# A split-precision decoder layer: the products with the weights' lower parts are issued behind those with the upper parts

## The chip, the cores and the metric

The kernel runs on one core of a Trainium2 chip. The metric is the device time of one execution in microseconds. A profile of one execution stands beside it; its span runs from the first to the last instruction of the program. The engines are named as in the profile: PE is TensorE (matrix products), PEld its weight loads, DVE is VectorE, ACT is ScalarE, POOL is GpSimd, SP issues most of the DMAs.

## What is computed

One decoder layer for 256 tokens with 2048 channels, in float32: a conditioned RMSNorm, an input projection to twelve wide parts, two kinds of attention (retention with 4 heads, HGRN2 with 8), their output projections, gates and a merge, and then a feed-forward block with a causal convolution and a down projection from 5632 channels. Cut to its products:

```python
h   = modulate(rms_norm(x, g_norm1), shift1, scale1)
p   = h @ w_in                                   # 2048 x 12288
y_a = (o_r * silu(rg)) @ w_ret_o                 # 1024 x 2048
y_b = (o_h * silu(hg)) @ w_hg_o                  # 1024 x 2048
x   = x + gate1 * ((sigmoid(ga) * y_a + sigmoid(gb) * y_b) @ w_out)
h2  = modulate(rms_norm(x, g_norm2), shift2, scale2)
u   = causal_depthwise_conv(h2 @ w_up, conv_w, conv_b)
a, b = split(u)
x   = x + gate2 * ((silu(a) * b) @ w_down)       # 5632 x 2048
out = rms_norm(x, g_final)
```

## The kernel before

**Split operands.** The products keep more bits than one pass of the reduced-precision type fp32r holds: each operand is split into an upper part, rounded to fp32r, and a lower part, the rest. A product of two split operands is made of three: upper by upper, upper by lower and lower by upper. The activations are split once (tiles `hT`, `og`, `mT`, `gs`): columns 0 to 255 of such a tile are the upper part for 256 tokens (`act[:, :T]`), columns 256 to 511 the lower part (`act[:, T:]`). The weights come from HBM in float32 and are split on the way, piece by piece.

**Pieces of weights.** A piece is a pair of k tiles (128 rows of the weight matrix each) by a group of 512 columns, or a single k tile where only one is left. `load` (L153) issues its DMA on SP into one of 12 buffers `raw`; `upper` (L159) has ACT round it into `wh` (L167); `rest` (L170) has DVE subtract that from `raw`, which gives `wl` (L172). There are four buffers each of `wh` and `wl`. `pieces` (L176) yields them one after another, and `products` (L213) has a function `mm` issue the products for each k tile as it comes.

**Two forms of product.** Where the result is to have tokens as rows, `mm_rows` (L190) is used: the activations are the stationary operand, a token tile of 128 at a time, and the 512 weight columns move. For each k tile and each of the two token tiles it issues three products into that token tile's own PSUM bank: L196 (upper activations, `wh`), L197 (upper activations, `wl`), L198 (lower activations, `wh`). Where the result is to have channels as rows, `mm_cols` (L200) is used: a block of 128 weight columns is stationary, and the 256 tokens move. For each k tile and each of four blocks it issues L209 (`wh`, upper), L210 (`wh`, lower), L211 (`wl`, upper); two blocks share a PSUM bank. A pair of k tiles is twelve products of 512 columns in `mm_rows`, and twenty-four of 256 columns in `mm_cols`.

**Stages.** (1) `run` starts with four column groups at k tiles 0 and 1, issued one k tile at a time (L800 to L819), while the rest of the activations is still being made. (2) The twelve attention groups (L836 to L864): column groups for the retention's and HGRN2's queries and keys, row groups for the values; few k tiles at a time, and in between. (3) Gates and branch gates as row groups (L874 to L893), while the attention itself runs as generators (`hgrn` L521, `retention` L700) whose steps `pump` (L127) puts between the pieces; their matrix products are small and stand between the pairs on PE. (4) The output projections (L897, L913, L931), rows. (5) The up projection (`up_group`, L1066), which has products of its own (L1081 with `wh`, L1083 with `wl`) and does not call `mm_rows` or `mm_cols`. (6) The down projection (`down`, L1104), rows.

**Order.** A planner in the tile framework lays down the order of instructions on each engine when the program is built: it takes what is ready by its own estimate, in program order, when several are. Instructions given to `pin` (L141) keep program order among themselves while `self.ordered` is set. The products of `mm_rows` and `mm_cols` are not pinned; products into the same PSUM bank keep their order. Buffers come free for the next writer when the last reader is done, so ACT's next `wh` waits for the last product that reads the old one.

**Held products.** With `hold`, the last k tiles of a group are not issued as they come, but kept in `held` and then issued for token tile 0 first and token tile 1 after (L223 to L225), so that the work on token tile 0 can start ahead. This is done in the last group of the output projection and in the last group of the down projection.

Of the kernel before, what the change touches and what calls it, by code (L numbers as in the profile page):

```python
# [19 lines left out]
P = 128  # L20
D = 2048
T = 256
NT = T // P
# [10 lines left out]
RESIDENT = 2  # L34
# [21 lines left out]
class Kernel:  # L56
# [130 lines left out]
            uppers[k // 2] = None  # L187
            yield [(k + j, wh[:, j, :], wl[:, j, :]) for j in range(m)]

    def mm_rows(self, ps, act, wh, wl, first, last, tiles=range(NT)):  # L190

        nc = self.nc
        for t in tiles:
            hi = act[:, t * P : (t + 1) * P]
            lo = act[:, T + t * P : T + (t + 1) * P]
            nc.tensor.matmul(ps[t], lhsT=hi, rhs=wh, start=first, stop=False)  # L196
            nc.tensor.matmul(ps[t], lhsT=hi, rhs=wl, start=False, stop=False)  # L197
            nc.tensor.matmul(ps[t], lhsT=lo, rhs=wh, start=False, stop=last)  # L198

    def mm_cols(self, ps, act, wh, wl, first, last):  # L200

        nc = self.nc
        hi, lo = act[:, :T], act[:, T:]
        for j in range(4):
            cs = slice(j * P, (j + 1) * P)

            opens = first and j % 2 == 0
            out = ps[j // 2][:, j % 2 * T : (j % 2 + 1) * T]
            nc.tensor.matmul(out, lhsT=wh[:, cs], rhs=hi, start=opens, stop=False, skip_group_check=True)  # L209
            nc.tensor.matmul(out, lhsT=wh[:, cs], rhs=lo, start=False, stop=False, skip_group_check=True)  # L210
            nc.tensor.matmul(out, lhsT=wl[:, cs], rhs=hi, start=False, stop=last, skip_group_check=True)  # L211

    def products(self, mm, ps, src, act, k0, kts, hold=0, first=True, last=True, gain=None):  # L213

        held = []
        for step in self.pieces(src[:, k0 : k0 + kts, :], kts, gain):
            for kt, wh, wl in step:
                if kt >= kts - hold:
                    held.append((kt, wh, wl))
                else:  # L220
                    mm(ps, act(k0 + kt), wh, wl, first and kt == 0, last and kt == kts - 1)
            self.pump(len(step) / 2)
        for t in range(NT if held else 0):  # L223
            for kt, wh, wl in held:
                mm(ps, act(k0 + kt), wh, wl, kt == 0, kt == kts - 1, [t])  # L225
        return ps

    def rows(self, src, act, k0=0, kts=KT, ps=None):
# [526 lines left out]
    def run(self):  # L755
        nc, a = self.nc, self.a
# [11 lines left out]
        def act(k):  # L768
            return hT[k // 2][:, k % 2, :]
# [13 lines left out]
        mms = [self.mm_rows if c0 in ROWS else self.mm_cols for c0 in ATT]  # L783
# [15 lines left out]
        ps = [self.po2(), self.po2(), self.pg(), self.pg()][:FIRST]  # L799
        for k in range(2):  # L800
            for i in range(4 if k else 1):
                if k and i == 1:
                    self.times(k, 1, rx)
                next(ada[k])
            if k == 0:
                self.times(k, 1, rx)

            ahead = 2 * k
            uppers = [self.upper(a["wa"][g][:, k : k + 1, :], 1, G) for g in range(ahead + 1)]
            rests = [self.rest(z) for z in uppers[:ahead]]  # L810
            for _ in ada[k]:
                pass
            for g in range(FIRST):
                if g >= ahead:
                    rests.append(self.rest(uppers[g] if g < len(uppers) else self.upper(a["wa"][g][:, k : k + 1, :], 1, G)))
                wh, wl = rests[g]
                if k == g == 0:
                    self.pin(nc.scalar.activation(rx_sb, rx, AF.Copy))
                mms[g](ps[g], act(k), wh[:, 0, :], wl[:, 0, :], k == 0, k == 1 and g >= RESIDENT)  # L819
        for _ in range(2):  # L820
            next(ada[2])
        self.ordered = False
# [10 lines left out]
        g = FIRST  # L833
        att, gates = [], []
        small = False
        while min(done) < KT:  # L836
# [25 lines left out]
            g = (g + 1) % len(ATT)  # L862
            if have == KT and done[0] < KT:
                g = min(i for i in range(len(ATT)) if done[i] < KT)  # L864
# [9 lines left out]
        for j in range(4):  # L874
            ps = self.rows(a["wb"][j], act)
# [55 lines left out]
        for j in range(4):  # L931
            last = j == 3
            x1.append(self.load_rows(j))
            if not last:
                g = self.row(self.gate["gate1"], j, "g1")
            if j == 2:
                g3 = self.row(self.gate["gate1"], 3, "g1")
            elif last:
                g = g3
            ps = self.products(self.mm_rows, self.po2() if last else self.pg(), a["wout"][j], actm, 0, KT, hold=4 * last, gain=g if last else None)  # L940
            if last:
                g = None
# [305 lines left out]
```

## Time and profile before

| | |
|---|---|
| median of 3 runs | 1516.57 us (1516.51 to 1517.36) |
| span of the profiled execution | 1514.7 us |
| PE busy | 1498.0 us |
| PEld busy | 1288.4 us |
| DVE busy | 1205.9 us |
| ACT busy | 845.4 us |

The profile's page gives no time of its own for the profiled execution beside its span; the median lies 1.87 us above that span. Busy times of one engine count overlapping instructions once. A weight load overlaps the product in front of it. In rows that list groups of instructions, the columns are line, engine, operation, written tile and read tiles, shape, count, then busy microseconds and mean nanoseconds of one, then the idle time of the engine ahead of them with what ended it. In the timeline, the first column is the start in microseconds from the beginning of the span and the second the time the rows take. In the table by stretches the columns are the length, then busy time and count of PE, PEld, DVE, ACT and POOL, the granted TensorE clock, the DMA share and GB/s.

### The profile page before, as it was taken

The page shows a single profiled execution, that of the slowest core. Times are in us where ns is not written, and L with a number is a line of the kernel's source. Part 1 is how long each engine was busy: PE and PEld are TensorE (multiplying, and loading weights), DVE is VectorE, ACT ScalarE, POOL GpSimd, SP SyncE. Part 2 cuts the span into 40 slices and gives each one's busy share as a digit, 9 for nine tenths or more (in the row PEclk, how much of TensorE's full clock was granted, in tenths as well). Part 3 has the DMA queues.
Part 4 walks back from the last instruction along what each step waited for, and adds up shares of the span by engine and source line. Part 5 has one row for each costly group of instructions (what it writes and reads, how often), then busy time and mean ns, then how long its engine had stood idle before and what let it go on. Part 6 is the DMA issues. An engine that isn't in the chain of part 4 may idle for free.

```text
span 1514.7 us, 23095 instructions
## 1 busy us (share of the span) xinstructions
PE 1498.0 (99%) x8722; PEld 1288.4 (85%) x8722; DVE 1205.9 (80%) x1639; ACT 845.4 (56%) x1207; POOL 4.0 (0%) x8
## 2 busy tenths in 40 slices
PE   8999999999999999999999999999999999999997
PEld 6999999878788888888888888888888888888886
DVE  7899996898999877898977778778777769455694
ACT  6645454768775644445466555555555558344343
POOL 0000000000000000000000000000000000000000
PEclk9999999999999999999999999999999999999999
DMA  9999997777888889989847777777777666667651
GB/s 376 377 344 332 316 325 228 229 275 266 287 264 289 275 288 329 320 289 358 310 133 242 237 230 233 228 233 231 230 245 228 220 187 196 201 209 215 177 178 56
DMA packets 110997, 385.75 MB, mean 255 GB/s; under 512 B 12803, under 2 KB 13347, under 8 KB 110885
## 3 DMA queue, kind: packets, MB, share of 16 engines
q1 hardware_dynamic: 110016, 383.14, 76.7%
q8 instruction: 68, 1.11, 0.3%
q10 hardware_dynamic: 868, 1.13, 0.2%
q14 instruction: 45, 0.36, 0.1%
HBM read 382.11 MB, written 2.11 MB: 254 GB/s over the span
## 4 chain that ended last, share of the span: by engine, by line
PE 95%; ACT 2%; DVE 1%; DMA 1%; issue 0%; SPq 0%; DVEq 0%; ACTq 0%
PE pg L196 13%; PE pg L197 13%; PE pg L198 13%; PE po L1081 11%; PE pg L1081 10%; PE po L1083 5%; PE pg L1083 5%; PE po L197 3%; PE po L198 3%; PE po L196 3%; PE pg L209 3%; PE pg L211 3%; PE pg L210 3%; PE po L209 1%; PE po L210 1%; PE po L211 1%
## 5 line engine op out<-in xcount | busy, mean ns | idle before, releaser
L167 ACT ACTIVATE wh<-raw 128x1024 fp32r<-128x1024 f32 (+1 forms) x536 | 550.6, 1033 | 523.2 <-PE pg L198 183.4
L172 DVE TENSOR_TENSOR wl<-raw,wh 128x1024 fp32r<-128x1024 f32 (+1 forms) x536 | 634.5, 1190 | 248.2 <-ACT wh L167 247.4
L421 DVE SCALAR_TENSOR_TENSOR raw<-raw,sc 128x1024 f32<-128x1024 f32 x192 | 233.5, 1219 | 0.0
L1081 PE MATMUL po<-h2T,wh 128*128 128x512 f32 x704 | 221.1, 395 | 0.0
L1081 PE MATMUL pg<-h2T,wh 128*128 128x512 f32 x688 | 216.4, 396 | 0.0
L196 PE MATMUL pg<-wh,hT 128*128 128x512 f32 x512 | 203.1, 397 | 0.2 <-ACT p L789 0.2
L197 PE MATMUL pg<-wl,hT 128*128 128x512 f32 x512 | 200.5, 392 | 1.7 <-DVE wl L172 1.7
L198 PE MATMUL pg<-wh,hT 128*128 128x512 f32 x512 | 199.6, 390 | 0.0
L1083 PEld LDWEIGHTS po<-h2T,wl 128*128 128x128 f32 x704 | 132.2, 188 | 31.3
L1083 PEld LDWEIGHTS pg<-h2T,wl 128*128 128x128 f32 x688 | 129.1, 188 | 31.0 <-DVE wl L172 0.5
L1083 PE MATMUL po<-h2T,wl 128*128 128x256 f32 x704 | 138.3, 278 | 0.0
L1083 PE MATMUL pg<-h2T,wl 128*128 128x256 f32 x688 | 135.3, 278 | 0.1
L197 PEld LDWEIGHTS pg<-wl,hT 128*128 128x128 f32 x512 | 96.2, 188 | 22.1 <-DVE wl L172 3.3
L198 PEld LDWEIGHTS pg<-wh,hT 128*128 128x128 f32 x512 | 96.1, 188 | 20.2
L196 PEld LDWEIGHTS pg<-wh,hT 128*128 128x128 f32 x512 | 96.2, 188 | 19.9 <-ACT p L789 0.4
L211 PE MATMUL pg<-hT,wl 128*128 128x256 f32 x384 | 109.0, 284 | 0.6 <-DVE wl L172 0.6
L209 PE MATMUL pg<-hT,wh 128*128 128x256 f32 x384 | 109.2, 284 | 0.1
L210 PE MATMUL pg<-hT,wh 128*128 128x256 f32 x384 | 109.0, 284 | 0.0
L1081 PEld LDWEIGHTS po<-h2T,wh 128*128 128x128 f32 x704 | 107.1, 189 | 0.0
L1081 PEld LDWEIGHTS pg<-h2T,wh 128*128 128x128 f32 x688 | 104.7, 189 | 0.0
L211 PEld LDWEIGHTS pg<-hT,wl 128*128 128x128 f32 x384 | 74.0, 193 | 0.8 <-DVE wl L172 0.8
L209 PEld LDWEIGHTS pg<-hT,wh 128*128 128x128 f32 x384 | 74.1, 193 | 0.6 <-ACT wh L167 0.2
(250 smaller groups left out, 2208.3 us busy)
## 6 DMA issues: line engine op xcount, KB each, us to landing
raw<-in_wup SPq DMA_DIRECT2D x176, 512.0 KB, 4.5
raw<-in_wdown SPq DMA_DIRECT2D x88, 512.0 KB, 4.3
raw<-in_wa SPq DMA_DIRECT2D x80, 512.0 KB, 6.0
raw<-in_ada SPq DMA_DIRECT2D x64, 512.5 KB, 5.7
raw<-in_ada SPq DMA_DIRECT2D x64, 512.0 KB, 5.8
raw<-in_wab SPq DMA_DIRECT2D x64, 512.0 KB, 5.1
raw<-in_gate SPq DMA_DIRECT2D x32, 512.5 KB, 4.8
raw<-in_wb SPq DMA_DIRECT2D x32, 512.0 KB, 5.0
```

What stands on the lines that cost most here:

```text
L167: self.pin(self.nc.scalar.activation(wh, raw, AF.Copy))
L172: self.last = self.nc.vector.tensor_tensor(wl, raw, wh.bitcast(F32), ALU.subtract)
L196: nc.tensor.matmul(ps[t], lhsT=hi, rhs=wh, start=first, stop=False)
L197: nc.tensor.matmul(ps[t], lhsT=hi, rhs=wl, start=False, stop=False)
L198: nc.tensor.matmul(ps[t], lhsT=lo, rhs=wh, start=False, stop=last)
L209: nc.tensor.matmul(out, lhsT=wh[:, cs], rhs=hi, start=opens, stop=False, skip_group_check=True)
L210: nc.tensor.matmul(out, lhsT=wh[:, cs], rhs=lo, start=False, stop=False, skip_group_check=True)
L211: nc.tensor.matmul(out, lhsT=wl[:, cs], rhs=hi, start=False, stop=last, skip_group_check=True)
L421: dot = self.pin(nc.vector.scalar_tensor_tensor(raw[:, 0, :], raw[:, 0, :], 1.0, self.sc[:, u * GW : u * GW + w], ALU.mult, ALU.mult, accu ...
L1081: self.pin(nc.tensor.matmul(ps[j + z], lhsT=wh[:, cs[z]], rhs=act, start=kt == 0, stop=False, skip_group_check=bool(begun)))
L1083: nc.tensor.matmul(ps[j + z][:, :T], lhsT=wl[:, cs[z]], rhs=act[:, :T], start=False, stop=kt == KT - 1, skip_group_check=bool(begun))
```

## The change

`mm_rows` and `mm_cols` take the k tiles of a piece together, as a list of items, instead of one k tile a call. They issue the products with `wh` first (with the activations' upper part and then the lower part), for all items and both token tiles or all four column blocks, and the products with `wl` behind them. `products` hands them the whole piece. The held products of a token tile are issued the same way, all with `wh` and then all with `wl`. The number of products, their operands and the banks that they add into are the same. `up_group` is not touched.

```diff
-    def mm_rows(self, ps, act, wh, wl, first, last, tiles=range(NT)):
+    def mm_rows(self, ps, items, first, last, tiles=range(NT)):
 
         nc = self.nc
         for t in tiles:
-            hi = act[:, t * P : (t + 1) * P]
-            lo = act[:, T + t * P : T + (t + 1) * P]
-            nc.tensor.matmul(ps[t], lhsT=hi, rhs=wh, start=first, stop=False)
-            nc.tensor.matmul(ps[t], lhsT=hi, rhs=wl, start=False, stop=False)
-            nc.tensor.matmul(ps[t], lhsT=lo, rhs=wh, start=False, stop=last)
+            hi, lo = [slice(u * T + t * P, u * T + (t + 1) * P) for u in range(2)]
+            for i, (act, wh, _) in enumerate(items):
+                nc.tensor.matmul(ps[t], lhsT=act[:, hi], rhs=wh, start=first and i == 0, stop=False)
+                nc.tensor.matmul(ps[t], lhsT=act[:, lo], rhs=wh, start=False, stop=False)
+        for t in tiles:
+            hi = slice(t * P, (t + 1) * P)
+            for i, (act, _, wl) in enumerate(items):
+                nc.tensor.matmul(ps[t], lhsT=act[:, hi], rhs=wl, start=False, stop=last and i == len(items) - 1)
...
-    def mm_cols(self, ps, act, wh, wl, first, last):
+    def mm_cols(self, ps, items, first, last):
 
         nc = self.nc
-        hi, lo = act[:, :T], act[:, T:]
-        for j in range(4):
-            cs = slice(j * P, (j + 1) * P)
-
-            opens = first and j % 2 == 0
-            out = ps[j // 2][:, j % 2 * T : (j % 2 + 1) * T]
-            nc.tensor.matmul(out, lhsT=wh[:, cs], rhs=hi, start=opens, stop=False, skip_group_check=True)
-            nc.tensor.matmul(out, lhsT=wh[:, cs], rhs=lo, start=False, stop=False, skip_group_check=True)
-            nc.tensor.matmul(out, lhsT=wl[:, cs], rhs=hi, start=False, stop=last, skip_group_check=True)
+        cs = [slice(j * P, (j + 1) * P) for j in range(4)]
+        outs = [ps[j // 2][:, j % 2 * T : (j % 2 + 1) * T] for j in range(4)]
+        for i, (act, wh, _) in enumerate(items):
+            for j in range(4):
+
+                opens = first and i == 0 and j % 2 == 0
+                nc.tensor.matmul(outs[j], lhsT=wh[:, cs[j]], rhs=act[:, :T], start=opens, stop=False, skip_group_check=True)
+                nc.tensor.matmul(outs[j], lhsT=wh[:, cs[j]], rhs=act[:, T:], start=False, stop=False, skip_group_check=True)
+        for i, (act, _, wl) in enumerate(items):
+            for j in range(4):
+                nc.tensor.matmul(outs[j], lhsT=wl[:, cs[j]], rhs=act[:, :T], start=False, stop=last and i == len(items) - 1, skip_group_check=True)
 
     def products(self, mm, ps, src, act, k0, kts, hold=0, first=True, last=True, gain=None):
 
         held = []
         for step in self.pieces(src[:, k0 : k0 + kts, :], kts, gain):
-            for kt, wh, wl in step:
-                if kt >= kts - hold:
-                    held.append((kt, wh, wl))
-                else:
-                    mm(ps, act(k0 + kt), wh, wl, first and kt == 0, last and kt == kts - 1)
+            items = [(act(k0 + kt), wh, wl) for kt, wh, wl in step]
+            kt = step[0][0]
+            if kt >= kts - hold:
+                held += items
+            else:
+                mm(ps, items, first and kt == 0, last and kt + len(step) == kts)
             self.pump(len(step) / 2)
         for t in range(NT if held else 0):
-            for kt, wh, wl in held:
-                mm(ps, act(k0 + kt), wh, wl, kt == 0, kt == kts - 1, [t])
+            mm(ps, held, hold == kts, True, [t])
         return ps
...
-                mms[g](ps[g], act(k), wh[:, 0, :], wl[:, 0, :], k == 0, k == 1 and g >= RESIDENT)
+                mms[g](ps[g], [(act(k), wh[:, 0, :], wl[:, 0, :])], k == 0, k == 1 and g >= RESIDENT)
```

## The prediction

> **What bounds the kernel now.** I read the page first: busy time, the chain that ended last, the groups.
>
> ```profile
> span 1514.7 us, 23095 instructions
> ...
> PE 1498.0 (99%) x8722; PEld 1288.4 (85%) x8722; DVE 1205.9 (80%) x1639; ACT 845.4 (56%) x1207; POOL 4.0 (0%) x8
> ...
> PE 95%; ACT 2%; DVE 1%; DMA 1%; issue 0%; SPq 0%; DVEq 0%; ACTq 0%
> ```
>
> TensorE is busy for 1498.0 of 1514.7 us and is 95% of the chain. The change removes no product and adds none, so two things can move the time: what one product costs, and the 16.7 us in which TensorE is idle, with what hides inside its busy time. For the first I read the groups with shapes kept apart.
>
> ```profile
> L198 PE MATMUL pg<-wh,gs 128*128 128x512 f32 x176 | 68.6, 390 | 0.0
> L196 PE MATMUL pg<-wh,gs 128*128 128x512 f32 x176 | 68.5, 389 | 0.0
> L197 PE MATMUL pg<-wl,gs 128*128 128x512 f32 x176 | 68.5, 389 | 0.0
> ```
>
> In the down projection nothing waits, and the three products of a k tile cost the same to 1 ns, whichever stands first and whichever operand it reads. A new order of the same three is therefore worth nothing by itself. For the second I read who waited for whom on PE, then the timeline around each wait for `wl`.
>
> ```profile
> PE pg L197 <- DVE wl L172: 1.7, 3, 0.8
> ...
> PE pg L211 <- DVE wl L172: 0.6, 1, 0.6
> ```
>
> That is 2.3 us in four waits, for the lower part of a weight piece, which DVE makes (L172) out of the upper part, which ACT makes (L167). The four places, PE alone:
>
> ```profile
> 38.34 0.28 PE L210 MATMUL pg<-hT,wh 128*128 128x256 f32 x1
> 39.17 0.39 PE L211 MATMUL pg<-hT,wl 128*128 128x256 f32 x1 [0.55 <-DVE wl L172]
> 39.40 0.28 PE L209 MATMUL pg<-hT,wh 128*128 128x256 f32 x1
> ...
> 281.74 0.28 PE L211 MATMUL pg<-hT,wl 128*128 128x256 f32 x1
> 281.86 0.39 PE L196 MATMUL pg<-wh,hT 128*128 128x512 f32 x1
> 282.73 0.50 PE L197 MATMUL pg<-wl,hT 128*128 128x512 f32 x1 [0.48 <-DVE wl L172]
> 283.07 0.39 PE L198 MATMUL pg<-wh,hT 128*128 128x512 f32 x1
> ...
> 375.68 0.39 PE L198 MATMUL pg<-wh,hT 128*128 128x512 f32 x1
> 375.90 0.39 PE L196 MATMUL pg<-wh,hT 128*128 128x512 f32 x1
> 376.66 0.50 PE L197 MATMUL pg<-wl,hT 128*128 128x512 f32 x1 [0.38 <-DVE wl L172]
> 377.00 0.40 PE L198 MATMUL pg<-wh,hT 128*128 128x512 f32 x1
> ...
> 384.73 0.39 PE L196 MATMUL pg<-wh,hT 128*128 128x512 f32 x1
> 385.93 0.50 PE L197 MATMUL pg<-wl,hT 128*128 128x512 f32 x1 [0.81 <-DVE wl L172]
> 386.26 0.39 PE L198 MATMUL pg<-wh,hT 128*128 128x512 f32 x1
> ```
>
> Starts, not durations, show the pace, as products overlap: undisturbed, a 512-column product starts 0.22 to 0.23 us after the one before (375.68 to 375.90) and a 256-column one 0.12 (281.74 to 281.86). I take 0.227 and 0.12. A stall costs more than its idle time, because the pipeline drains and the product behind the stalled one starts 0.33 to 0.34 us later instead of 0.227. From starts: at 39 us 0.83 - 0.12 and 0.23 - 0.12, together 0.82; at 282 us 0.87 - 0.23 and 0.34 - 0.23, 0.75; at 376 us 0.76 - 0.23 and 0.34 - 0.23, 0.64; at 385 us 1.20 - 0.23 and 0.33 - 0.23, 1.07. **Sum 3.28 us.** The rest of the idle time is the start-up (before 17 us, and small waits for hT), the hand-over to the up projection and what follows the last product: none of it waits for `wl`.
>
> **The change part by part.** *Order inside a pair.* In mm_rows the first product with `wl` was second of twelve; it becomes ninth, 7 x 0.227 = 1.59 us later after the pair's start. In mm_cols with a pair it goes from third to seventeenth, 14 x 0.12 = 1.68 us. The four waits last 0.38 to 0.81 us, so all would be covered if `wl` comes when it comes now: -3.28 us. Ends for this term: 2.3 us (idle time alone) and 3.28. I take 3.28, since the drag behind each stall is in the rows.
>
> *What is late next.* The tightest place is the last. If the wait at 376 us goes, the pairs start at 375.90, 378.62, 381.34 and 384.06 (12 x 0.227 = 2.72 us each); the fourth is the one that started at 384.73. It needs this:
>
> ```profile
> 382.94 1.04 ACT L167 ACTIVATE wh<-raw 128x1024 fp32r<-128x1024 f32 x1
> ```
>
> ```profile
> 384.67 1.20 DVE L172 TENSOR_TENSOR wl<-raw,wh 128x1024 fp32r<-128x1024 f32 x1
> ```
>
> `wh` is done at 383.98, 0.08 us ahead of 384.06; `wl` at 385.87, where the ninth product comes at 384.06 + 1.82 = 385.88. So this place is covered with nothing to spare. It stays out of the sum, and makes a rival.
>
> *Buffers.* `wh` is read for the last time at product 8 of 12 instead of 12 of 12, so its buffer comes free 4 x 0.227 = 0.91 us sooner; ACT waits for just that:
>
> ```profile
> ACT wh L167 <- PE pg L198: 183.4, 131, 2.6
> ```
>
> `wl` is read until product 12 instead of 11, 0.23 us later. DVE does not feel it: it needs the new `wh` too, which with 1.04 us of ACT ends at 1.82 + 1.04 = 2.86 us, behind the pair's end at 2.72. In a stretch where TensorE never waits the earlier `wh` is worth nothing; before an attention burst it is up to 0.9 us more lead. Below nothing it can only go through the planner (third rival). The loads on SP's queue go by `raw`, which DVE frees after `wl`, at most 0.9 us sooner: nothing, as no product waits for them.
>
> *Tokens' lower part.* In mm_rows it is needed second instead of third, 0.23 us sooner. No product of a row group waits for it, so 0. act() of a pair's second tile is called ahead of the first tile's products; each call that emits work emits it for the whole pair already, so nothing moves.
>
> *Held pieces, end.* For one token tile the held products are the same in number; the last starts where it did. Up projection (L1081, L1083): untouched. 0.
>
> *Stationary operand.* L196 and L197 load the same tokens one behind the other; the new order separates them.
>
> ```profile
> L197 PEld LDWEIGHTS pg<-wl,hT 128*128 128x128 f32 x512 | 96.2, 188 | 22.1 <-DVE wl L172 3.3
> ```
>
> There are as many loads as products (8722 each), L197's are not shorter for following L196, and 188 ns lie under a pace of 227: 0. The Trainium skill, "TensorE: Matmul & The Clock Gate", section "Step-by-step: what each phase is for", speaks against the change here: weights that stay put are to be loaded once and multiplied repeatedly. By that rule 1120 spared loads would be lost, at 188 ns 211 us if they stood in the open; the trace spares none today.
>
> *Sum.* 1514.7 - 3.3 = 1511.4 for the profiled execution. The median of the runs, 1516.57, lies 1.87 us above the span; the same distance gives **1513.3**, 0.22% less. About 0.2%, 3.0 us, is what a measurement of this kernel can tell from no change, so the forecast stands on that line.
>
> **The rivals.** *The wait comes back as a wait for `wh`* (0.32). For: the margins of 0.08 and 0.01 us above; a product that is late at the start of a pair is not helped by the new order. If the waits at 376 and 385 us return in full, 0.64 + 1.07 are lost again and 1.57 stays: 1515.0. Against: `wh` buffers come free sooner.
>
> *It does nothing* (0.08): the planner that lays down each engine's order puts the products back, or lead gained at a place is used up by the next burst: 1516.6.
>
> *Slower: DVE's order* (0.15). The planner works with its own estimate of when a buffer comes free. Sooner free `wh` changes which of ACT's and DVE's instructions come first, and attention work can land ahead of a `wl`. DVE has no room there:
>
> ```profile
> 425.00:450.00 25.00, 25.00 (x295) 20.04 (x294) 24.82 (x31) 16.46 (x26) 0.00 (x0) 1.00 0.77 236
> ...
> 800.00:825.00 25.00, 25.00 (x145) 21.80 (x145) 18.53 (x28) 15.23 (x23) 0.00 (x0) 1.00 0.73 240
> ```
>
> 24.82 of 25 us at 425 us, against 18.53 in the up projection. One level of the attention's tree puts at least these two on DVE:
>
> ```profile
> L590 DVE TENSOR_TENSOR e<-b 128x1024 f32<-128x1024 f32 x10 | 12.0, 1215 | 0.0
> L519 DVE COPY_PREDICATED at<-lmask,po 128x512 f32<-128x512 int32 x10 | 9.7, 967 | 1.1 <-PE po L613 1.1
> ```
>
> 1.22 + 0.97 = 2.2 us ahead of a `wl` that is just in time costs a mean of 3.28 / 4 + 2.2 - 1.59 = 1.43 us. At four places 5.7 us stand for today's 3.3: 1519.0. It decides from 1.59 us at all four. Against: program order puts that attention work where it stood.
>
> *A rule on banks* (0.02 with the rule on loads). In mm_cols a pair goes to another PSUM bank 8 times instead of 4. If that throttled the clock, the products would go at the pace of the cold start:
>
> ```profile
> 18.01 0.41 PE L209 MATMUL po<-hT,wh 128*128 128x256 f32 x1
> 18.23 0.41 PE L210 MATMUL po<-hT,wh 128*128 128x256 f32 x1
> ```
>
> 0.22 instead of 0.12 us for 1536 products is +154 us: 1670. Against: L1081 changes bank at every product, at the granted clock of 1.00 and 145 products in 25 us (row 800 above). The Trainium skill's page "TensorE: Matmul & The Clock Gate", section "A second HAM failure mode: psum-queue depth-cycling", tells of cycling through banks that makes the clock oscillate; by that rule this rival, against which the trace speaks.
>
> **How the numbers follow.** Forecast 0.43 (1513.3; its own range 1511.8 to 1514.3, below by lead gained elsewhere, above by the 2.3 us end); it falls below 1513.5 with 0.36 and within 0.2% with 0.07. Faster 0.36; same 0.07 + 0.32 + 0.08 = 0.47; slower 0.15 + 0.02 = 0.17. The range runs from 1511.8 to 1518.5: it takes in the forecast, both rivals without a loss and the near half of the slower one.
>
> **What would show it.** Right: no PE wait for DVE `wl` in the row and column products, PE idle about 2.2 us less, and the pace of 0.227 and 0.12 us unbroken at the four places. If PE waits for ACT `wh` near 380 us in its place, the first rival. If DVE's instructions between 280 and 480 us come in another order, with a new wait of over 1.4 us, the third. Wrong from the ground: a product whose mean duration in the down projection is not 389.

## The result and the profile after

| | before | after |
|---|---|---|
| median of 21 runs each | 1516.53 us | 1513.86 us |
| lowest to highest | 1516.06 to 1517.49 | 1513.51 to 1515.23 |
| span of the profiled execution | 1514.7 us | 1512.0 us |

The ratio is 0.9983 (95% interval 0.9977 to 0.9989): the changed kernel is 0.17% faster, 2.67 us by the medians, clear of no change and just inside the 0.2% line. In the changed kernel the line numbers behind L222 are 5 higher; in `mm_rows` L196 is upper activations by `wh`, L197 lower by `wh`, L201 upper by `wl`; in `mm_cols` these are L212, L213 and L216.

The page after, in the same rows as before:

```profile
span 1512.0 us, 23190 instructions
...
PE 1496.0 (99%) x8722; PEld 1288.2 (85%) x8722; DVE 1206.4 (80%) x1639; ACT 846.6 (56%) x1207; POOL 4.0 (0%) x8
...
PE 95%; DVE 3%; DMA 1%; ACT 1%; issue 0%; SPq 0%; DVEq 0%; ACTq 0%
```

TensorE's count is unchanged, its busy time 2.0 us less; idle time, 16.0 us against 16.7, fell by only 0.7 where the prediction looked for about 2.2. That is the first hint that something was given back. The waits of PE after, three rows of them:

```profile
PE pg L1065 <- DVE h2T L398: 0.7, 1, 0.7
PE po L618 <- DVE kt L602: 0.6, 1, 0.6
PE pg L212 <- DVE p L796: 0.6, 1, 0.6
```

No wait of PE for `wl` is left in row and column products. The first row was there before (the hand-over to the up projection). The two others are new: a small attention product (L618) waits for DVE's `kt`, and a column product (L212) for DVE's accumulation out of PSUM (`p`, L796).

**The four stalls are gone.** The tightest place of before (384.73 to 385.93 us there), in the timeline of the changed kernel on PE, DVE and ACT:

```profile
383.97 0.39 PE L197 MATMUL pg<-wh,hT 128*128 128x512 f32 x1
384.20 1.14 PE L201 MATMUL pg<-wl,hT 128*128 128x512 f32 x4
385.17 0.39 PE L196 MATMUL pg<-wh,hT 128*128 128x512 f32 x1
```

```profile
382.88 1.20 DVE L172 TENSOR_TENSOR wl<-raw,wh 128x1024 fp32r<-128x1024 f32 x1
```

```profile
381.15 1.05 ACT L167 ACTIVATE wh<-raw 128x1024 fp32r<-128x1024 f32 x1
```

The pair starts at 382.38 (eight products of 0.227 ahead of 384.20). `wh` is ready at 382.20, 0.18 us before that, and `wl` at 384.08, 0.12 us before the first product that reads it. The prediction had margins of 0.08 and 0.01 us here. The margins were nearly used up all the same: the weight load that stands in front of a product waits with it, and in the changed kernel the loads at 382.25 and 384.14 us waited 0.13 us for `wh` and 0.21 us for `wl`. The second product with `wl` starts 0.28 us behind the first instead of 0.227, a loss of 0.05 us; the others follow at a pace of 0.23 to 0.24.

**A fifth wait that PE's rows do not show.** Before the change the loads of L197 waited for `wl` five times, and only three of these waits appear as idle time of PE. The row of the waits, then PE and the load at the place that matters:

```profile
PEld pg L197 <- DVE wl L172: 3.3, 5, 1.2
```

```profile
444.43 0.39 PE L196 MATMUL pg<-wh,hT 128*128 128x512 f32 x1
444.75 0.50 PE L197 MATMUL pg<-wl,hT 128*128 128x512 f32 x1
445.09 0.39 PE L198 MATMUL pg<-wh,hT 128*128 128x512 f32 x1
```

```profile
444.75 0.19 PEld L197 LDWEIGHTS pg<-wl,hT 128*128 128x128 f32 x1 [0.36 <-DVE wl L172]
```

The load waited 0.36 us while the product ahead of it still counted as busy. From start to start that costs 0.32 - 0.227 and 0.34 - 0.227, 0.21 us, and the wait is gone after the change. The other hidden one, at 120 us, costs about 0.02 us.

**What was given back at the attention.** The timeline of PE after, around the two places where an attention product waits:

```profile
423.37 0.39 PE L196 MATMUL pg<-wh,hT 128*128 128x512 f32 x1
424.40 0.73 PE L618 MATMUL po<-eq,kt 128*32 128x16 f32 x64 [0.64 <-DVE kt L602]
425.06 0.50 PE L197 MATMUL pg<-wh,hT 128*128 128x512 f32 x1
...
435.39 0.39 PE L196 MATMUL pg<-wh,hT 128*128 128x512 f32 x1
435.85 0.76 PE L658 MATMUL po<-eq,kt 128*32 128x32 f32 x64
436.54 0.50 PE L197 MATMUL pg<-wh,hT 128*128 128x512 f32 x1
```

A burst of small products that waits for nothing starts 0.32 us behind the wide product ahead of it (328.07 to 328.39 in the rows further below). Here it is 1.03 and 0.46: 0.71 + 0.14 = 0.85 us lost. The planner now puts these two bursts inside a pair, the first behind its seventh product and the second behind its first, where they stood between pairs before; they wait there for `kt` and `eq`. DVE's instruction that they wait for, in the timeline before and after:

```profile
424.24 0.68 DVE L597 TENSOR_TENSOR kt<-e,k 128x512 f32<-128x512 f32 x1
```

```profile
423.58 0.67 DVE L602 TENSOR_TENSOR kt<-e,k 128x512 f32<-128x512 f32 x1
```

DVE is done 0.67 us sooner than before, while PE, relieved of its stalls, stood there 1.8 us sooner: the burst that began at 425.47 before could have begun at 423.69 and began at 424.40, after a wait. DVE could not follow: it has no idle time between 400 and 450 us and hardly any up to 475 (25.00, 25.00 and 24.96 us busy in the three stretches of 25 us).

**What was given back at 280 us.** DVE's order changed. Its timeline before, then after:

```profile
277.25 1.22 DVE L791 TENSOR_TENSOR p<-p,pg 128x1024 f32<-128x1024 f32 x1 [1.50 <-PE pg L198]
278.39 0.68 DVE L172 TENSOR_TENSOR wl<-raw,wh 128x512 fp32r<-128x512 f32 x1
278.99 2.54 DVE L791 TENSOR_TENSOR p<-p,pg 128x1024 f32<-128x1024 f32 x2
```

```profile
276.48 1.22 DVE L796 TENSOR_TENSOR p<-p,pg 128x1024 f32<-128x1024 f32 x1 [0.90 <-PE pg L201]
277.61 1.22 DVE L172 TENSOR_TENSOR wl<-raw,wh 128x1024 fp32r<-128x1024 f32 x1
278.75 2.35 DVE L796 TENSOR_TENSOR p<-p,pg 128x1024 f32<-128x1024 f32 x2
```

A whole `wl` (1.22 us) stands ahead of the two accumulations where half a one (0.68) stood; the accumulation frees the PSUM bank that PE needs next, and that product starts 0.77 us late at 280.11, where a stall of 0.23 us stood at that place before: +0.53.

**What came on top.** Before the change two bursts of the attention's small products were split over two pairs, and each part pays its own way out of the wide products and back. The timeline of PE before, at the first part of one of them, and after, where the burst stands in one:

```profile
328.07 0.39 PE L196 MATMUL pg<-wh,hT 128*128 128x512 f32 x1
328.39 0.32 PE L613 MATMUL po<-eq,kt 128*32 128x16 f32 x16
328.63 0.50 PE L197 MATMUL pg<-wl,hT 128*128 128x512 f32 x1
328.97 0.39 PE L198 MATMUL pg<-wh,hT 128*128 128x512 f32 x1
```

```profile
329.87 0.74 PE L618 MATMUL po<-eq,kt 128*32 128x16 f32 x64
330.54 0.50 PE L196 MATMUL pg<-wh,hT 128*128 128x512 f32 x1
330.87 0.39 PE L197 MATMUL pg<-wh,hT 128*128 128x512 f32 x1
```

Sixteen products took 0.90 us from 328.07 to 328.97 where two wide ones take 0.45. Both parts together cost 1.17 us beyond the wide products' pace, the whole burst 0.86: 0.31 us saved, twice (the other split stood at 335 and 338 us). Both bursts are whole in every kernel below with a new order in the rows, and both are split with a new order in the columns alone; why the planner joins them is not shown.

**The account:** -3.28 (four stalls), -0.21 (the fifth), -0.62 (splits), +0.85 (attention), +0.53 (280 us), +0.05 (384 us) and +0.13 at 41 us, where a column product's load, coming sooner, waits for the tokens' lower part `hT` from DVE: -2.55. PE's last product starts 2.78 us sooner than before (1503.90 against 1506.68), of which 0.07 lie ahead of the first stall; some 0.2 us of small gains are not assigned.

### The profile page after: what moved, and what is told of

It is laid out like the page before. It is cut to its first block, busy times and chain, and to the rows that moved or that the text cites. A ratio compares the mean times of both kernels' runs of the same rounds, so it can differ in the third digit from the quotient of the medians.

```text
span 1512.0 us, 23190 instructions
## 1 busy us (share of the span) xinstructions
PE 1496.0 (99%) x8722; PEld 1288.2 (85%) x8722; DVE 1206.4 (80%) x1639; ACT 846.6 (56%) x1207; POOL 4.0 (0%) x8
## 4 chain that ended last, share of the span: by engine, by line
PE 95%; DVE 3%; DMA 1%; ACT 1%; issue 0%; SPq 0%; DVEq 0%; ACTq 0%
PE pg L196 13%; PE pg L197 13%; PE pg L201 13%; PE po L1086 11%; PE pg L1086 10%; PE po L1088 5%; PE pg L1088 5%; PE po L201 3%; PE po L197 3%; PE po L196 3%; PE pg L212 3%; PE pg L213 3%; PE pg L216 3%; PE po L212 1%; PE po L213 1%; PE po L216 1%
## 5 line engine op out<-in xcount | busy, mean ns | idle before, releaser
L196 PE MATMUL pg<-wh,hT 128*128 128x512 f32 x512 | 202.8, 396 | 0.2 <-ACT p L794 0.2
L197 PE MATMUL pg<-wh,hT 128*128 128x512 f32 x512 | 200.0, 391 | 0.0
L201 PE MATMUL pg<-wl,hT 128*128 128x512 f32 x512 | 137.4, 390 | 0.0
L201 PEld LDWEIGHTS pg<-wl,hT 128*128 128x128 f32 x512 | 96.0, 188 | 20.4 <-DVE wl L172 0.2
L196 PEld LDWEIGHTS pg<-wh,hT 128*128 128x128 f32 x512 | 96.2, 188 | 19.9 <-ACT p L794 0.4
L197 PEld LDWEIGHTS pg<-wh,hT 128*128 128x128 f32 x512 | 96.2, 188 | 19.1
L212 PE MATMUL pg<-hT,wh 128*128 128x256 f32 x384 | 95.2, 284 | 0.6 <-DVE p L796 0.6
L213 PE MATMUL pg<-hT,wh 128*128 128x256 f32 x384 | 95.1, 284 | 0.0
L212 PEld LDWEIGHTS pg<-hT,wh 128*128 128x128 f32 x384 | 74.1, 193 | 1.1 <-issue 0.8
L213 PEld LDWEIGHTS pg<-hT,wh 128*128 128x128 f32 x384 | 74.0, 193 | 0.3
L197 PE MATMUL pg<-wh,gs 128*128 128x512 f32 x176 | 68.6, 390 | 0.0
```

The source lines that it names most:

```text
L196: nc.tensor.matmul(ps[t], lhsT=act[:, hi], rhs=wh, start=first and i == 0, stop=False)
L197: nc.tensor.matmul(ps[t], lhsT=act[:, lo], rhs=wh, start=False, stop=False)
L201: nc.tensor.matmul(ps[t], lhsT=act[:, hi], rhs=wl, start=False, stop=last and i == len(items) - 1)
L212: nc.tensor.matmul(outs[j], lhsT=wh[:, cs[j]], rhs=act[:, :T], start=opens, stop=False, skip_group_check=True)
L213: nc.tensor.matmul(outs[j], lhsT=wh[:, cs[j]], rhs=act[:, T:], start=False, stop=False, skip_group_check=True)
```

## The experiments

Theory 1: the gain is that `wl` is needed later in the piece. Theory 2: the gain is that `wh` comes free sooner, so that ACT and DVE run further ahead. Both halves are in the change, and each can be had alone. Times below are medians beside the kernel before on the same chip; the ratio stands with its 95% interval. The start-up alone moves a single execution: before_dots, whose products stand as in the kernel before up to there, starts the product that stands at 36.41 us, ahead of the first stall, 0.73 us later than that kernel does. Where a time in the text is said to be behind the start-up, this shift is taken off the start of PE's last product in the profiled execution; it is -2.71 us for the changed kernel.

| kernel | us | before | ratio |
|---|---|---|---|
| wh_kept | 1513.63 | 1516.59 | 0.9978 (0.9968 to 0.9987) |
| wl_early | 1515.69 | 1516.59 | 0.9991 (0.9983 to 1.0000) |
| rows_only | 1515.01 | 1516.59 | 0.9986 (0.9978 to 0.9995) |
| cols_only | 1515.98 | 1516.59 | 0.9995 (0.9986 to 1.0004) |
| per_kt | 1513.95 | 1516.83 | 0.9981 (0.9972 to 0.9989) |
| dots_later | 1512.95 | 1516.83 | 0.9974 (0.9964 to 0.9983) |
| wh_kept_dots | 1513.55 | 1516.83 | 0.9976 (0.9968 to 0.9985) |
| wh_kept_dots_up | 1515.50 | 1516.83 | 0.9994 (0.9985 to 1.0003) |
| after_b | 1513.97 | 1516.88 | 0.9982 (0.9973 to 0.9990) |
| dots_b | 1513.00 | 1516.88 | 0.9975 (0.9965 to 0.9985) |
| before_dots | 1516.62 | 1516.88 | 0.9996 (0.9988 to 1.0005) |
| dots_up1 | 1516.02 | 1516.88 | 0.9990 (0.9973 to 1.0007) |

### wl later, wh not sooner

In these two kernels the order is written out as lists; `lows` are the products with `wl`, `order` those with `wh`, and `order + lows` stands for the changed kernel's order.

```diff
 # in mm_rows and mm_cols
-        order = order + lows
+        order = order[:-1] + lows + order[-1:]
```

> Order of the changed kernel, except that the last product with wh of each piece is issued behind the products with wl, so that ACT's wh buffer comes free at the piece's end as before the change, while wl is needed as late as in the changed kernel (eighth of twelve products instead of ninth). Theory 1 (the gain is wl being needed later): no PE wait for DVE wl in row and column products, 2 to 3 us below the kernel before, span near 1512.5. Theory 2 (the gain is wh coming free sooner, so that ACT and DVE run further ahead): at least two of the four waits for wl come back or turn into waits for ACT wh, and the time is within 1 us of the kernel before, 1515.5 to 1516.5.

Measured: 1513.63 us, 2.96 below the kernel before; no wait of PE for `wl` in row and column products. (A load waits for it, 0.44 us at 383.96 us, and costs 0.29 us from start to start: `wl` is needed one product sooner here than in the changed kernel.) Of the changed kernel's two new waits, the one at 280 us is down from 0.61 to 0.08 us with the old order of DVE, and the attention's is shorter. DVE's timeline, then the wait:

```profile
276.74 1.22 DVE L799 TENSOR_TENSOR p<-p,pg 128x1024 f32<-128x1024 f32 x1 [1.50 <-PE pg L202]
277.88 0.69 DVE L172 TENSOR_TENSOR wl<-raw,wh 128x512 fp32r<-128x512 f32 x1
278.48 2.54 DVE L799 TENSOR_TENSOR p<-p,pg 128x1024 f32<-128x1024 f32 x2
```

```profile
PE po L621 <- DVE kt L605: 0.4, 1, 0.4
```

Half a `wl` stands ahead of the accumulations, as before the change. So theory 1 holds and theory 2 falls: the whole gain is there without `wh` coming free sooner (-3.34 us behind the start-up). And the sooner free `wh` is what moved DVE's order at 280 us.

### wh sooner, wl not later

```diff
 # mm_rows; in mm_cols the first two of order stand ahead
-        order = order + lows
+        order = order[:1] + lows[:1] + order[1:] + lows[1:]
```

> The other half alone: the first product with wl stands where it stood before the change (second of twelve in rows, third in columns), the others with wl are issued at the end, so that wh comes free at product nine of twelve. Theory 1: the waits for wl at the four places come back, 0.4 to 0.8 us of idle time each, and the time is within 1 us of the kernel before, near 1516. Theory 2: ACT and DVE run ahead by 0.7 us more, the waits of 0.38 to 0.55 us vanish, and 2 us or more of the gain stay, near 1514.

Measured: 1515.69 us, 0.90 below the kernel before. All products of `mm_rows` have line L202 here, those of `mm_cols` L219. Waits of PE:

```profile
PE pg L202 <- DVE wl L172: 1.0, 2, 0.8
PE pg L1068 <- DVE h2T L401: 0.7, 1, 0.7
PE pg L219 <- DVE p L799: 0.6, 1, 0.6
PE pg L219 <- DVE wl L172: 0.6, 1, 0.6
```

Three of the four waits for `wl` are back (0.27 and 0.77 us at 376 and 385 us, 0.55 near 39 us); the one of 282 us is not, and the wait for the accumulation near 280 us stands in its place. The sooner free `wh` is worth little: 0.11 and 0.05 us off the two waits at 376 and 385, and the 0.05 may not be its doing, as cols_only below, with the old order in the rows, has the same 0.77 us there. Most of what this kernel gains is the two whole bursts (0.62 us). Expected was about 1516.

### Rows alone, columns alone

In each, one of the two functions loops as before the change over the k tiles of the piece, with `wl` inside.

> New order in mm_rows alone; mm_cols as before the change. Theory 1: the three row stalls (0.75, 0.64 and 1.07 us) go and the one at 39 us (0.82) stays: 1.5 to 2.5 us below the kernel before, near 1514.5. If the loss at 280 us in the changed kernel (a wait of PE for DVE's accumulation out of PSUM, 0.5 us more than before) belongs to the column order, it is absent here, and the time can be as low as that of the changed kernel. Theory 2 gives about the same and is not told apart by this run.

Measured: 1515.01 us, 1.58 below. The waits at 282, 376 and 385 us are gone, the one at 39 us stays (0.55 us). The waits at 280 us (0.61) and at the attention (0.65 and 0.08) are there as in the changed kernel, so they come with the row order; the expectation that the first could belong to the column order fell.

> New order in mm_cols alone; mm_rows as before the change. Theory 1: the stall at 39 us (0.82) goes, the three row stalls stay (2.46 us together): 0.3 to 0.9 us below the kernel before, near 1516. A wait near 280 us for DVE's accumulation out of PSUM of about 0.6 us if that belongs to the column order.

Measured: 1515.98 us, 0.61 below (the interval takes in no change). The stall at 39 us is gone, the three row stalls stay, and there is no wait at 280 us. The two halves give 1.58 + 0.61 = 2.19 us of the 2.67: they add up within what the runs can tell. Behind the start-up they are -2.13 and -0.71, together -2.84 beside -2.71.

### A smaller delay of wl

```diff
-                mm(ps, items, first and kt == 0, last and kt + len(step) == kts)
+                for i, item in enumerate(items):
+                    mm(ps, [item], first and kt + i == 0, last and kt + i == kts - 1)
```

> The changed kernel's order inside each k tile alone: the products with wl stand behind those with wh of the same k tile, not of the whole piece. The first product with wl of a row pair is then fifth of twelve, 0.68 us later than before the change instead of 1.59. Theory 1 (the gain follows the delay of the first wl): the waits of 0.38, 0.48 and 0.55 us go, about 0.13 us of the one of 0.81 stays; 2 to 3 us below the kernel before. If the gain came from all wh products being together, or from wh free much sooner (here at product ten of twelve), it is half of that or less.

Measured: 1513.95 us, 2.88 below, as forecast; but not in the way forecast. One wait for `wl` is left in the rows, in the profile's list of waits of PE, and it is five times the 0.13 us expected:

```profile
PE pg L201 <- DVE wl L172: 0.7, 1, 0.7
```

It stands at 384.88 us. The expectation took the lateness of before, 0.81, less the delay of 0.68. But the stall at 376 us (0.64) ahead of it is gone, so PE comes that much sooner: 0.81 - 0.68 + 0.64 = 0.77; 0.66 was measured. In return the wait at the attention, 0.64 us in the changed kernel, is not there: PE is held up at 385 us instead of at 424. The time is that of the changed kernel. What is saved at one place is partly a wait at the next, as long as DVE's work in between takes as long.

### Less work on DVE where PE waits for it

```diff
-        self.pace(1, 68.0, 96)
+        self.pace(1, 25.0, 56)
...
         for j in range(8):
+            if j == 3:
+                self.pace(1, 43.0, 40)
             gt = self.blk([P, NT, G], name="gt")
```

> The changed kernel with one more edit: DVE's dot products for the gates (L426 there) are paced slower until the third branch gate and faster after it, the same number in all. Theory on the new waits at 424 and 436 us (0.64 and 0.06 us idle, PE for DVE kt and eq): they stand where DVE has no idle time, and PE, no longer held up earlier, comes to the attention's products too soon. Then with fewer dots on DVE they vanish: 0.5 to 1.2 us below the changed kernel, near 1513.0. Rival: the waits come from ACT's table loads or from the place where the planner puts the attention's products; then they stay, and the time is that of the changed kernel within 0.4 us. The wait near 280 us stays in either case.

Measured: 1512.95 us, 3.88 below the kernel before. Neither attention product waits any more. DVE and PE between 425 and 450 us, in the table by stretches, for the changed kernel and for this one (from its second profile, dots_b):

```profile
425.00:450.00 25.00, 24.94 (x247) 20.35 (x236) 25.00 (x33) 16.43 (x28) 0.00 (x0) 1.00 0.79 246
```

```profile
425.00:450.00 25.00, 25.00 (x236) 20.45 (x235) 21.14 (x29) 17.34 (x27) 0.00 (x0) 1.00 0.79 253
```

DVE's 25.00 of 25 us fall to 21.14. In the stretch from 400 to 425 us, where the longer wait stood, it is 25.00 and 24.68; what differs is the work ahead of it, as the dot products take 17.33 us between 350 and 425 us in the changed kernel and 11.07 here. The `kt` ahead of the first burst, which ended at 424.25 us, now ends at 421.86, and the burst does not wait although PE reaches it sooner (dots_b, DVE and PE):

```profile
421.16 0.70 DVE L602 TENSOR_TENSOR kt<-e,k 128x512 f32<-128x512 f32 x1
```

```profile
422.15 0.39 PE L197 MATMUL pg<-wh,hT 128*128 128x512 f32 x1
422.47 0.73 PE L618 MATMUL po<-eq,kt 128*32 128x16 f32 x64
```

The planner has moved this burst five products up the stream as well. That alone could not have ended the wait: against the old `kt` an earlier place would wait longer. Beside the changed kernel on one chip it ran once more:

> The changed kernel once more, on the same chip as the next two: 2.3 to 3.1 us below the kernel before.

> The changed kernel with the dots paced later, once more, beside the changed kernel. If its 0.9 us are those of the two waits at 424 and 436 us, it stays 0.5 to 1.2 us below the changed kernel here.

Measured: 1513.97 and 1513.00 us. The medians differ by 0.97 us, near the 0.85 that the two waits cost from start to start, and behind the start-up the two differ by 0.83 us (-3.53 against -2.70); the intervals of the ratios to the kernel before overlap, so it is the trace that shows the cause. This kernel has the lowest median of those here, 0.9975 of the time before.

> The kernel before the change with the dots paced later alone. Theory: before the change PE is held up by wl ahead of the attention's products, so DVE's dots cost little there; the waits at 376 and 385 us stand behind ACT's burst of table loads, which this edit does not touch. Within 0.8 us of the kernel before. Rival: the dots alone hold DVE up and the whole gain could be had by pacing them; then 2 us or more below it.

Measured: 1516.62 against 1516.88 us, no difference that the runs can tell; all four waits of PE for `wl` are there (1.5 us in rows, 0.6 in columns). So the new order does not merely repair what pacing could have repaired: the pacing is worth something only once the order of the products has brought PE forward.

### Both repairs, and the up projection

> Both edits that each take away one of the changed kernel's new waits: wh kept to the end of the piece (DVE's order near 280 us as before the change) and the dots paced later. If the two losses are separate, both vanish: 0.5 to 1.5 us below the changed kernel, near 1512.8.

Measured: 1513.55 us. In the trace both waits are gone (0.08 us is left at 280 us), and the profiled execution has the shortest span of all, 1510.7 us; behind the start-up it is at -3.98 us, beside -3.34 for wh_kept and -3.53 for dots_b. But its eleven runs spread from 1512.27 to 1514.34, and the median is no lower than with the dots alone. That the two repairs add up shows in one execution's trace and not in the medians.

```diff
-                for j in range(0, 4, 2):
-                    cs = [slice(z * P, (z + 1) * P) for z in (j, j + 1)]
-                    for z in range(2):
+                cs = [slice(z * P, (z + 1) * P) for z in range(4)]
+                for z in range(4):
...
-                    for z in range(2):
+                for z in range(4):
```

> As the one before, and in the up projection the four products with wl of a k tile are issued behind the four with wh. One wait is there for wl, 0.11 us of idle time and 0.28 us from start to start, in the first group. If it goes: 0.2 to 0.3 us less than the kernel before in this list, less than the runs can tell; the trace shows it. If the pace of the 5632 products of this stage depends on their order (now 0.23 and 0.12 us), the time moves by more than 1 us.

Measured: 1515.50 us, 1.95 above the kernel without this edit, and its lowest run (1514.74) is above the highest of that one. (The stage has 2784 products of the two widths; the 5632 of the expectation is wrong.) The wait for `wl` at 790 us is gone, and the stage is longer all the same: 489.62 us from its first to its last product instead of 486.57. Products of PE in the same 425 us, before the change and here (table by stretches):

```profile
800.00:1225.00 425.00, 425.00 (x2442) 370.82 (x2442) 322.39 (x483) 239.11 (x362) 0.00 (x0) 1.00 0.73 231
```

```profile
800.00:1225.00 425.00, 425.00 (x2425) 371.40 (x2424) 317.85 (x481) 234.38 (x358) 0.00 (x0) 1.00 0.72 228
```

2425 products in place of 2442, at the full granted clock. From start to start a narrow product behind a narrow one takes 118.6 ns here and 114.7 two by two.

> The changed kernel with the dots paced later, and in the up projection each product with wl straight behind the product with wh of the same block (one by one instead of two by two). Four by four was 3.0 us longer in this stage (489.62 against 486.57 us from its first to its last product) with one wait less. If narrow products in a row are what costs (118.6 instead of 114.7 ns from start to start), one by one is 1 to 4 us shorter still, less about 0.5 us for an earlier wait for wl in the first group. If two by two is the best mix, it is longer by 1 us or more.

Measured: the median of 1516.02 us says little, for the twelve executions fall into two groups of six, 1511.07 to 1512.19 and 1519.84 to 1521.15 us. The profiled execution is one of the second (span 1518.0), with 2408 products in the same stretch. What sets which group an execution falls into is open. In the second group one by one is slower than two by two: 493.79 us from the first to the last product. The first group is the lowest seen here, has no trace, and is not explained. So the expectation is neither met nor refuted.

## Why the prediction was right, and where it was off

- **An order of the same three products is worth nothing by itself.** Right for this change, whose products stand among products of the same width. In the down projection after (groups with shapes kept apart):

```profile
L197 PE MATMUL pg<-wh,gs 128*128 128x512 f32 x176 | 68.6, 390 | 0.0
L196 PE MATMUL pg<-wh,gs 128*128 128x512 f32 x176 | 68.5, 389 | 0.0
```

  The same 389 to 390 ns. It is not a general rule: in the up projection, where wide and narrow ones alternate, four by four cost 3.0 us.
- **Four stalls, 3.28 us.** Right in place, kind and size: all four went, and wl_early brought three of them back. The second source of doubt, idle time alone (2.3 us) or from start to start (3.28), can't be settled from the total, but the trace can settle it: over the two places at 376 and 385 us PE gains 1.7 us on the kernel before, which is the 0.64 + 1.07 from start to start, where the idle time alone is 1.2. The list of waits was not complete: reading PE's rows alone left out the wait that the load hid at 444.75 us (0.21 us). Nor is it so that no other idle time waits for `wl`: the up projection has 0.11 us at 794 us, which this change leaves alone.
- **What is late next: `wh`.** The rival with 0.32 did not come, but narrowly: margins of 0.18 and 0.12 us were left at the tightest place, and the loads there already waited 0.13 and 0.21 us.
- **Buffers: below nothing only through the planner.** Right, and it happened: the sooner free `wh` moved a `wl` ahead of two accumulations at 280 us, +0.53 us, shown by wh_kept and wl_early. The slower rival's mechanism was real; its price of 1.43 us at each of four places was not reached, because it struck one place, and not one where `wl` was late; no new wait was over 1.4 us.
- **The step that failed** is the one that took the stalls' sum for the gain ("all would be covered if `wl` comes when it comes now: -3.28 us"). It looked for the next late operand of the same pair, and not for the next engine down the stream: the attention's products, standing in PE's order where DVE has no idle time, gave back 0.85 us, and a load waiting for DVE's `hT` at 41 us another 0.13. PE's idle time, forecast to fall by about 2.2 us, fell by 0.7. The row that showed DVE at 24.82 of 25 us was in hand, and was used for the slower rival alone.
- **Not foreseen and in favour:** two split bursts that became whole, 0.62 us, and the fifth wait, 0.21 us. That these 0.83 us made up for a good half of the 1.56 us given back is luck, and with it that the time came out only 0.6 us above the forecast.
- **The rules of the Trainium skill.** L196 and L201 no longer load the same tokens one behind the other, and the weight load is what it was:

```profile
L201 PEld LDWEIGHTS pg<-wl,hT 128*128 128x128 f32 x512 | 96.0, 188 | 20.4 <-DVE wl L172 0.2
```

  The Trainium skill's "TensorE: Matmul & The Clock Gate", section "Step-by-step: what each phase is for", says that one load of a stationary operand can serve many products. To order the products against that cost nothing here, as no load was spared before. Column products, which now go to another bank twice as often, keep their 284 ns (L212) at a granted clock of 1.00 (275 to 300 us). The oscillation of the clock that the Trainium skill's "TensorE: Matmul & The Clock Gate" tells of in its section "A second HAM failure mode: psum-queue depth-cycling" did not show.

## What to carry to other kernels

Where the first operand of a piece is ready long before the second, issue everything that needs the first ahead of everything that needs the second: it costs no instruction, and it can cover a wait about as long as what is moved ahead takes (1.59 us here, of which the tightest place used all but 0.12). Read the waits of the weight loads beside those of the products, as a load can hide one. Count the gain from start to start and then go down the stream: an engine that arrives sooner waits at the next engine that has no idle time, and that wait, not the sum of the stalls removed, sets what is kept. A buffer that comes free sooner also reorders the engines that fill it, which is not always a gain.

## What the runs showed of the hardware

- A product that was held up by a wait costs more than the wait: from start to start 0.16 us beyond the idle time of the stalled product, and 0.10 to 0.11 us more at the next. With 2.2 us of idle time in the four stalls, 1.1 us were such drag. A wait can also cost time without any idle time of PE: the load that waited 0.36 us at 444.75 us cost 0.21.
- Going from wide products to a burst of small ones and back costs about 0.31 us per burst whatever its size, an estimate from two bursts before the change: 16 of the small products cost 0.45 us beyond the wide products' pace and 64 cost 0.86, by which one product is 0.0085 us and the rest is the way in and out. A split burst pays it twice.
- The pace of TensorE depends on the order of widths where products of 512 and 256 columns alternate: blocks of four wide and four narrow took 3.0 us longer over 2784 products than two and two. The order is not all, as one by one gave two groups of times 9 us apart with the same program. The Trainium skill's page "TensorE: Matmul & The Clock Gate", section "Back-to-back issue gap", says that in a stream of load and product pairs the spacing is set by both. No run here shows how much of the 114.7 and 118.6 ns is the load's share.
